# Attention in a fused decoder layer: where the value matmuls of a half are issued, and in which tile the last block's exponentials lie

## The chip, the core and the metric

The kernel runs on one core of one Trainium2 chip. The metric is the device time of one execution in microseconds, the median of several runs. Five engines work side by side, each in its own instruction order: TensorE (PE) for matmuls, VectorE (DVE), ScalarE (ACT) and GpSimd (POOL) for element-wise work, and SyncE (SP), which issues most DMAs. They wait for each other through semaphores.

## What is computed

One decoder layer on a sequence of 1024 tokens with 1024 channels: a state-space branch (SSD) and a latent-attention branch (MLA), merged by gates, then a gated feed-forward part. Everything is float32 in and out. The change touches the attention alone, which is, for 16 heads (64 value columns each, 96 query and key columns):

```python
def one_block(i):
    start = i * ATTN_Q_BLOCK
    qb = lax.dynamic_slice_in_dim(q, start, ATTN_Q_BLOCK, axis=1)
    s = jnp.einsum('bqhd,bkhd->bhqk', qb, k).astype(jnp.float32) * scale
    qpos = start + jnp.arange(ATTN_Q_BLOCK)
    s = jnp.where(qpos[:, None] >= key_pos[None, :], s, -jnp.inf)
    p = jax.nn.softmax(s, axis=-1).astype(v.dtype)
    return jnp.einsum('bhqk,bkhd->bqhd', p, v)
```

## The kernel before

The layer runs as stages one after the other: normalisation and small projections, the attention stage (about 105 to 697 us of the profiled execution), the SSD, the merge, the feed-forward part. In the attention stage PE's free places are filled with background work: the gate and z projections, whose matmuls write a PSUM tile `lin`. One background step is three lin matmuls of 512 columns (a product of two split numbers, high and low parts in fp32r). `advance(n)` issues n steps; `fill()` issues as many as the next digit of the table `PACE` says, so each call of `fill` uses up one place of the table. What is left of the background after the attention is issued by `flush()`.

Heads are worked in 8 pairs, and the 1024 queries in two halves of 512. A first half (half 0) has 4 key blocks of 128 keys, a second half 8. For each key block and head, `key_block` makes scores transposed (keys on the partitions, queries in the columns) with three matmuls into an `s` bank, adds the causal mask on DVE where the block is on the diagonal (L657), takes the exponential on ACT into a tile `e` (L659) and adds e to a running sum `acc`, head 0 on POOL, head 1 on DVE (L664). Of the last four blocks of a half, block number d (0 to 3) has only 512 - 128 d columns that count, so e is 512, 384, 256 and 128 columns wide. `values` then multiplies e with the values, one matmul for each head, both into one `pv` tile, head 0 in its upper 64 rows and head 1 in its lower ones (L670). These matmuls are plain float32 and 64 columns of the array wide. `output` adds acc over the partitions with a matmul against ones (L677), copies pv and the sums out on ACT and stores them by DMA from SP.

Ahead of the scores each pair needs its projections (`qkv_steps`, with a reciprocal square root in many small DVE instructions and the qk scalings L586 and L588), transposes to kh, kl, qh, ql (`qk_transposed`, L610 on PE, L613 on ACT, L614 on DVE) and the negative maxima of the scores (`maxima`: L627 matmuls, DVE reductions L629 and L632 into nm, mc at L637 or L639, and L643 matmuls). These are the side work: in a first half the second half's transposes and maxima, in a second half the next pair's projections, transposes and maxima. `aside` issues it by the counts of `SIDE`. All `s` tiles, those of the side work too, rotate through 4 PSUM banks; `e` tiles rotate through 6 buffers, of which the output's sums take one.

A finished key block goes on a queue. When the queue holds more than two blocks, `value_steps` takes the two oldest and issues their value matmuls; behind a half's last two it also issues the output. So the last two blocks of a half are multiplied after the first key block of the next half.

On PE the order of the program is the order of the code: a chain of order marks over all of PE's instructions fixes it. On the other engines a scheduler places instructions when the kernel is built, so that a changed PE order moves theirs too.

Of the kernel before, what the change touches and what calls it, by code (L numbers as in the profile page):

```python
# [9 lines left out]
F32 = mybir.dt.float32  # L10
F32R = mybir.dt.float32r
I32 = mybir.dt.int32
AF = mybir.ActivationFunctionType
ALU = mybir.AluOpType
# [3 lines left out]
P = 128  # L18
# [54 lines left out]
def tile_hybrid_layer(ctx: ExitStack, tc: tile.TileContext, x, cols, cons, w_main, w_small, w_uq, w_ukv,  # L73
                      w_ssd, w_mla, w_o, w_up, w_down, out, pace=PACE):
    nc = tc.nc
    V, S, G, PE = nc.vector, nc.scalar, nc.gpsimd, nc.tensor
# [130 lines left out]
    def advance(n):  # L207
        while n > 0 and background:
            r = next(background[0], None)
            if r is None:  # L210
                background.pop(0)
            elif not r:
                return
            else:
                n -= 1

    def fill():
        i = places[0]
        places[0] += 1
        advance(int(pace[i], 36) if i < len(pace) else 0)  # L220
# [216 lines left out]
    for half in range(2):  # L437
        for b in range(3):
            fill()
            ps = bps.tile([P, 512], F32, name="tps")  # L440
# [15 lines left out]
    for tab, c0 in ((rq, CG_QR), (rk, CG_KR)):  # L456
# [21 lines left out]
    e = bq.tile([P, NT, HEADS], F32, name="de")  # L478
    u = bq.tile([P, NT, HEADS], F32, name="du")
    V.tensor_tensor(v, sm[:, :, 0:32], cl[:, CG_DTB:CG_DTB + 32].unsqueeze(1).broadcast_to([P, NT, 32]),  # L480
                    op=ALU.add)
# [19 lines left out]
    ps = bps.tile([P, 512], F32, name="tps")  # L501
    PE.matmul(ps[:, 0:256], lhsT=tri, rhs=va, start=True, stop=True)
    S.copy(acum.rearrange("p t h -> p (t h)"), ps[:, 0:256])
    ps = bps.tile([P, 512], F32, name="tps")
# [11 lines left out]
    for half in range(2):  # L516
        fill()
        ps = bps.tile([P, 512], F32, name="tps")
# [7 lines left out]
    with tc.tile_pool(name="cp", bufs=2) as cp, tc.tile_pool(name="pss", bufs=4, space=PSUM) as pss, \  # L526
# [119 lines left out]

        def key_block(pr, half, j, hd, accs):

            c0 = max(0, j - 4 * half) * P
            w = 512 - c0  # L650
            qh, ql = qkvT[pr, half, hd, "q"]
            kh, kl = qkvT[pr, j // 4, hd, "k"]
            ks = slice((j % 4) * P, (j % 4 + 1) * P)
            ps = bank()
            mm3(ps[:, 0:w], (kh[:, ks], kl[:, ks]), (qh[:, c0:512], ql[:, c0:512]), True, True)
            if j >= 4 * half:
                V.tensor_tensor(ps[:, 0:P], ps[:, 0:P], negt, op=ALU.add)  # L657
            e = cp.tile([P, 512], F32, name="e", bufs=6)
            S.activation(e[:, c0:512], ps[:, 0:w], AF.Exp)  # L659
            if j == 0:  # L660
                accs.append(cp.tile([P, 512], F32, name="acc"))
                S.copy(accs[hd], e)
            else:
                (V if hd else G).tensor_tensor(accs[hd][:, c0:512], accs[hd][:, c0:512], e[:, c0:512], op=ALU.add)  # L664
            return e

        def values(pr, j, es, c0, pv, first, last):
            vt = qkv[pr][1]
            for hd in range(2):
                PE.matmul(pv[hd * 64:(hd + 1) * 64, c0:512], lhsT=vt[:, j, hd * 64:(hd + 1) * 64],  # L670
                          rhs=es[hd][:, c0:512], start=first, stop=last)

        def output(pr, half, accs, pv):

# [32 lines left out]
        def attention():  # L707


            for g, n in ((qkv_steps(0), 10), (transposes(0, 0), 4), (both(0, 0), 10)):  # L710
                for _ in range(n):
                    fill()
                    next(g, None)
            queue = []

            def value_steps():

                done = [queue.pop(0) for _ in range(2)]
                last = done[1][2] == 4 * done[1][1] + 3
                if last:  # L720
                    fill()
                for pr, half, j, es, pv, accs in done:
                    values(pr, j, es, max(0, j - 4 * half) * P, pv, j == 0, j == 4 * half + 3)
                if last:
                    output(pr, half, accs, pv)

            units = 0
            for pr in range(npair):
                for half in range(2):
                    if half == 0:  # L730
                        side = chain(transposes(pr, 1), both(pr, 1))
                    elif pr + 1 < npair:
                        side = chain(qkv_steps(pr + 1), transposes(pr + 1, 0), both(pr + 1, 0))
                    else:
                        side = iter(())
                    todo = iter(SIDE[half])

                    def aside():
                        for _ in range(next(todo)):
                            fill()  # L740
                            next(side, None)


                    pv = psv.tile([P, 512], F32, name="pv")
                    accs = []
                    for j in range(4 * half + 4):
                        es = []
                        for hd in range(2):
                            fill()
                            es.append(key_block(pr, half, j, hd, accs))  # L750
                            aside()
                        queue.append((pr, half, j, es, pv, accs))
                        units += 1
                        if units > 2:
                            fill()
                        if len(queue) > 2:
                            value_steps()
                        aside()
                    for _ in side:
                        fill()  # L760
            fill()
            fill()
            value_steps()

        attention()
        flush()
# [887 lines left out]
```

## Time and profile before

| | us |
|---|---|
| median of 3 timed runs | 2227.03 (2224.92 to 2229.38) |
| the profiled execution | 2224.44 |
| its span in the trace | 2222.6 |
| PE's granted clock in it | 0.996 |
| value matmuls (L670), busy | 72.9 in 384 records |
| scores in pieces of 512 columns, first matmul (L175), busy | 40.1 in 96 records |

In the timeline a row has the start in us, how long it lasted, engine, line, operation, output<-inputs, sizes, count, and in brackets how long the engine sat idle before it and for whom. Matmuls overlap in these records (the shown end of one lies behind the start of the next), so that the distance from start to start says what one costs. A plain float32 matmul appears as two records, so a group of four value matmuls has x8. A row of a wait table has the total in us, the times, and the longest.

### The profile page before, as it was taken

How to read it: one execution, taken by the hardware profiler on the slowest of the kernel's cores; microseconds unless marked ns; L12 is line 12 of the kernel's file. 1: busy time of each engine (PE TensorE's matmuls, PEld its weight loads, DVE VectorE, ACT ScalarE, POOL GpSimd, SP SyncE). 2: the span in 40 equal slices, each digit the busy share in tenths (PEclk: the TensorE clock that was granted, in tenths of full speed). 3: DMA queues.
4: the chain of work that ended last, by engine and by line, in shares of the span. 5: the costliest groups of instructions: out<-in, count | busy, mean ns of one | idle time of the engine just before them, and what ended most of it. 6: DMA issues, size and time to landing. Idle time of an engine off the chain costs nothing.

```text
span 2222.6 us, 31323 instructions
## 1 busy us (share of the span) xinstructions
PE 2173.7 (98%) x11488; PEld 1765.2 (79%) x11488; DVE 1430.4 (64%) x2496; ACT 1012.4 (46%) x1852; POOL 822.4 (37%) x911
## 2 busy tenths in 40 slices
PE   8999999999999999999999999999899999999999
PEld 6777777777777887878878889889688888888887
DVE  4466656666672469898876746546977777764432
ACT  5345454445444346666554424335544444443320
POOL 2244423443343237665455311012555555510000
PEclk9999999999999999999999999999999999999999
DMA  4121111111213224544276566543222222247531
GB/s 146 54 68 49 40 48 63 50 45 39 69 43 130 68 76 152 181 162 167 95 227 207 178 223 203 166 162 95 67 95 86 81 81 86 76 142 246 201 130 67
DMA packets 112714, 253.57 MB, mean 114 GB/s; under 512 B 13168, under 2 KB 19248, under 8 KB 112560
## 3 DMA queue, kind: packets, MB, share of 16 engines
q1 hardware_dynamic: 99008, 210.54, 28.6%
q0 software_dynamic: 11008, 37.76, 5.3%
q10 hardware_dynamic: 2544, 3.28, 0.4%
q8 instruction: 90, 1.47, 0.3%
q14 instruction: 64, 0.52, 0.1%
HBM read 194.63 MB, written 56.89 MB: 113 GB/s over the span
## 4 chain that ended last, share of the span: by engine, by line
PE 75%; DVE 13%; ACT 4%; DMA 3%; issue 2%; POOL 1%; SPq 0%; DVEq 0%; ACTq 0%; POOLq 0%
PE lin L175 12%; PE lin L177 12%; PE lin L176 12%; PE dps L177 8%; PE dps L175 8%; PE dps L176 8%; PE pv L670 2%; PE s L175 2%; PE s L176 1%; PE s L177 1%; PE s L627 1%; PE yp L891 1%; PE sn L874 1%; DMA wraw<-in_w_ssd 1%; DVE qk L588 1%
## 5 line engine op out<-in xcount | busy, mean ns | idle before, releaser
L175 PE MATMUL lin<-h,whi 128*128 128x512 f32 x1440 | 592.4, 411 | 0.0
L177 PE MATMUL lin<-h,wlo 128*128 128x512 f32 x1440 | 564.0, 392 | 0.0
L176 PE MATMUL lin<-h,whi 128*128 128x512 f32 x1440 | 563.0, 391 | 0.0
L175 PEld LDWEIGHTS lin<-h,whi 128*128 128x128 f32 x1440 | 271.4, 188 | 81.6 <-issue 33.4
L177 PEld LDWEIGHTS lin<-h,wlo 128*128 128x128 f32 x1440 | 270.7, 188 | 59.8 <-DVE wlo L154 0.2
L176 PEld LDWEIGHTS lin<-h,whi 128*128 128x128 f32 x1440 | 271.9, 189 | 53.2 <-issue 7.0
L153 ACT CAST whi<-wraw 128x512 fp32r<-128x512 f32 x276 | 166.6, 619 | 281.4 <-PE lin L176 131.6
L154 POOL TENSOR_TENSOR wlo<-wraw,whi 128x512 fp32r<-128x512 f32 x134 | 192.1, 1450 | 185.1 <-ACT whi L153 177.6
L659 ACT ACTIVATE e<-s 128x512 f32<-128x512 f32 (+1 forms) x192 | 93.7, 493 | 164.6 <-DVE s L657 137.7
L664 POOL TENSOR_TENSOR acc<-acc,e 128x512 f32<-128x512 f32 (+3 forms) x80 | 79.6, 995 | 230.8 <-ACT e L659 217.7
L154 DVE TENSOR_TENSOR wlo<-wraw,whi 128x512 fp32r<-128x512 f32 x142 | 99.2, 714 | 94.4 <-ACT whi L153 94.3
L154 DVE TENSOR_TENSOR h<-ar,h 128x1024 fp32r<-128x1024 f32 x40 | 48.7, 1225 | 108.8 <-ACT h L153 108.7
L850 ACT ACTIVATE seg<-abc,acum 128x128 f32<-128x128 f32 x256 | 80.6, 392 | 48.3 <-PE yp L891 42.3
L153 ACT CAST h<-ar 128x1024 fp32r<-128x1024 f32 x40 | 42.1, 1056 | 124.8 <-PE lin L176 115.7
L176 PE MATMUL dps<-wlo,h 128*128 128x512 f32 x240 | 93.4, 389 | 0.0
L175 PE MATMUL dps<-whi,h 128*128 128x512 f32 x240 | 93.4, 389 | 0.0
L177 PE MATMUL dps<-whi,h 128*128 128x512 f32 x240 | 93.4, 389 | 0.0
L812 DVE SCALAR_TENSOR_TENSOR xg<-craw,cl,xg 128x1024 f32<-128x1024 f32 x48 | 73.8, 1537 | 27.4 <-ACT xg L810 26.9
L664 DVE TENSOR_TENSOR acc<-acc,e 128x512 f32<-128x512 f32 (+3 forms) x80 | 53.5, 668 | 41.0 <-ACT e L659 40.4
L1140 ACT CAST xhi<-ur 128x512 fp32r<-128x512 f32 (+1 forms) x41 | 34.1, 832 | 89.5 <-PE dps L176 79.5
L670 PE MATMUL pv<-e,vt 128*64 128x512 f32 (+3 forms) x384 | 72.9, 499 | 0.0
L175 PE MATMUL s<-qh,kh 97*128 97x512 f32 (+1 forms) x192 | 68.5, 357 | 2.0 <-ACT qh L644 1.1
(587 smaller groups left out, 5189.5 us busy)
## 6 DMA issues: line engine op xcount, KB each, us to landing
wraw<-in_w_main SPq DMA_DIRECT2D x112, 256.0 KB, 3.1
ur<-in_w_up SPq DMA_DIRECT2D x44, 512.0 KB, 3.5
ar<-a_d SPq DMA_DIRECT2D x40, 512.0 KB, 5.1
abc<-ac_d POOLq DMA_DIRECT2D x32, 512.0 KB, 5.2
wraw<-in_w_ssd SPq DMA_DIRECT2D x64, 256.0 KB, 2.8
wraw<-in_w_down SPq DMA_DIRECT2D x44, 256.0 KB, 3.8
a_d<-uc SPq DMA_DIRECT2D x22, 512.0 KB, 2.6
g_d<-lt SPq DMA_DIRECT2D x32, 256.0 KB, 2.8
```

Source lines behind the costliest of these rows:

```text
L153: S.copy(hi, raw)
L154: (eng or V).tensor_sub(lo, raw, hi.bitcast(F32))
L175: PE.matmul(ps, lhsT=ah, rhs=bh, start=first, stop=False, **more)
L176: PE.matmul(ps, lhsT=ah, rhs=bl, start=False, stop=False, **more)
L177: PE.matmul(ps, lhsT=al, rhs=bh, start=False, stop=last, **more)
L588: V.tensor_tensor(qk[:, :, 2 + hd, 0:64], qk[:, :, 2 + hd, 0:64], rr[:, :, 2 + hd:3 + hd].broadcast_to([P, 4, 64]), op=ALU.mult)
L659: S.activation(e[:, c0:512], ps[:, 0:w], AF.Exp)
L664: (V if hd else G).tensor_tensor(accs[hd][:, c0:512], accs[hd][:, c0:512], e[:, c0:512], op=ALU.add)
L670: PE.matmul(pv[hd * 64:(hd + 1) * 64, c0:512], lhsT=vt[:, j, hd * 64:(hd + 1) * 64], rhs=es[hd][:, c0:512], start=first, stop=last)
L812: V.scalar_tensor_tensor(c, raw[:, k:k + T], col(cw + k), c, op0=ALU.mult, op1=ALU.add)
L850: S.activation(seg[:, hd, :], abc[:, hd, :], AF.Relu, bias=acum[:, c, 8 * g + hd:8 * g + hd + 1], scale=-1.0)
L1140: S.copy(hi, r)
```

## The change

The value matmuls are issued in other groups. A first half has one group with all four blocks at its end. A second half has groups after its third and fifth block (blocks 0 and 1, blocks 2 and 3) and one of its last four blocks at its end. The output follows the last group, so a half's output now stands ahead of the next half's first key block. In a second half `advance(1)` puts one more background step ahead of the last group, whatever the table says. The `fill` ahead of an output becomes a `fill` at a half's first block, so that the table's places meet the same points of the code as before; the two fills at the very end go.

The last block's e (128 columns) no longer takes a tile of its own. It goes into the first 128 columns of the second diagonal block's tile, of which that block uses only the other 384.

```diff
-            c0 = max(0, j - 4 * half) * P
+            d = max(0, j - 4 * half)
+            c0 = d * P
...
-            e = cp.tile([P, 512], F32, name="e", bufs=6)
-            S.activation(e[:, c0:512], ps[:, 0:w], AF.Exp)
+
+            if d < 3:
+                e = cp.tile([P, 512], F32, name="e", bufs=6)
+                if d == 1:
+                    shared.append(e)
+                e = e[:, c0:512]
+            else:
+                e = shared.pop(0)[:, 0:w]
+            S.activation(e, ps[:, 0:w], AF.Exp)
...
-            def value_steps():
-
-                done = [queue.pop(0) for _ in range(2)]
-                last = done[1][2] == 4 * done[1][1] + 3
-                if last:
-                    fill()
+            def value_steps(n):
+
+                done = [queue.pop(0) for _ in range(n)]
+                last = n == 4
...
-                        if len(queue) > 2:
-                            value_steps()
+                        if units > 4 and j == 0:
+                            fill()
+                        if half and j in (2, 4):
+                            value_steps(2)
                         aside()
                     for _ in side:
                         fill()
-            fill()
-            fill()
-            value_steps()
+                    advance(half)
+                    value_steps(4)
```

Lines behind the edit move: L657 is L658 in the changed kernel, L659 is L667, L664 is L672, L670 is L680 and L677 is L687.

First place: PE where pair 2's second half ends and pair 3's first half begins. Before, the last two blocks' values stand behind the next half's first key block and its transposes (L610):

```order
L610 MATMUL s<-cn,qk 97x128 x4
L175 MATMUL s<-qh_3604,kh_3563 128x512
L176 MATMUL s<-ql_3605,kh_3563 128x512
L177 MATMUL s<-qh_3604,kl_3564 128x512
L610 MATMUL s<-cn,qk 97x128 x4
L670 MATMUL pv<-e,vt 64x256 x2
L670 MATMUL pv<-e,vt 64x128 x2
L677 MATMUL s<-acc,cn 32x256 x4
L175 MATMUL lin<-h,whi 128x512
```

In the changed kernel the last key block (its s matmuls of 128 columns), one background step, and then all four blocks' values and the output's sums:

```order
L175 MATMUL s<-qh_3049,kh_3020 128x128
L176 MATMUL s<-ql_3050,kh_3020 128x128
L177 MATMUL s<-qh_3049,kl_3021 128x128
L175 MATMUL lin<-h,whi 128x512
L176 MATMUL lin<-h,whi 128x512
L177 MATMUL lin<-h,wlo 128x512
L680 MATMUL pv<-e,vt 64x512 x2
L680 MATMUL pv<-e,vt 64x384 x2
L680 MATMUL pv<-e,vt 64x256 x2
L680 MATMUL pv<-e,vt 64x128 x2
L687 MATMUL s<-acc,cn 32x256 x4
```

The values and the ones matmul have moved ahead of the next half, and the transposes there no longer have them as a neighbour.

Second place: DVE in pair 2's second half, where the next pair's ql (both heads, L614) and the qk scalings (L586, L588) meet. Before:

```order
L614 SCALAR_TENSOR_TENSOR ql_3587<-s,qg,qh_3586 97x512
L586 TENSOR_TENSOR qk<-qk,qrr 128x4x96
L588 TENSOR_TENSOR qk<-qk,qrr 128x4x64
L586 TENSOR_TENSOR qk<-qk,qrr 128x4x96
L588 TENSOR_TENSOR qk<-qk,qrr 128x4x64
L614 SCALAR_TENSOR_TENSOR ql_3605<-s,qg,qh_3604 97x512
L657 TENSOR_TENSOR s<-s,negt 128x128
```

In the changed kernel, at the same place:

```order
L586 TENSOR_TENSOR qk<-qk,qrr 128x4x96
L588 TENSOR_TENSOR qk<-qk,qrr 128x4x64
L586 TENSOR_TENSOR qk<-qk,qrr 128x4x96
L588 TENSOR_TENSOR qk<-qk,qrr 128x4x64
L614 SCALAR_TENSOR_TENSOR ql_3583<-s,qg,qh_3582 97x512
L658 TENSOR_TENSOR s<-s,negt 128x128
L614 SCALAR_TENSOR_TENSOR ql_3601<-s,qg,qh_3600 97x512
```

The first ql has moved behind the four scalings, and the second behind a mask addition too. In pair 4's second half the second ql has moved behind the scalings in the same way, and in pair 5's a product of the background (L330) no longer stands ahead of them.

Third place: PE in pair 3's first half, behind the third key block, among the maxima of the second half (L627). Before:

```order
L627 MATMUL s<-kh_3563,qh_3858 128x512
L627 MATMUL s<-kh_3811,qh_3858 128x256
L670 MATMUL pv<-e,vt 64x512 x2
L670 MATMUL pv<-e,vt 64x384 x2
L175 MATMUL lin<-h,whi 128x512
L176 MATMUL lin<-h,whi 128x512
L177 MATMUL lin<-h,wlo 128x512
L627 MATMUL s<-kh_3537,qh_3838 128x512
```

In the changed kernel:

```order
L627 MATMUL s<-kh_3559,qh_3859 128x512
L627 MATMUL s<-kh_3827,qh_3859 128x256
L175 MATMUL lin<-h,whi 128x512
L176 MATMUL lin<-h,whi 128x512
L177 MATMUL lin<-h,wlo 128x512
L627 MATMUL s<-kh_3547,qh_3839 128x512
```

The value group between the maxima is gone; only the background step is left between them.

More of the change, by code (lines that the diff above doesn't have):

```diff
@@ L663, in key_block @@
             else:
-                (V if hd else G).tensor_tensor(accs[hd][:, c0:512], accs[hd][:, c0:512], e[:, c0:512], op=ALU.add)
+                (V if hd else G).tensor_tensor(accs[hd][:, c0:512], accs[hd][:, c0:512], e, op=ALU.add)
             return e
+        shared = []
         def values(pr, j, es, c0, pv, first, last):
@@ L670, in values @@
                 PE.matmul(pv[hd * 64:(hd + 1) * 64, c0:512], lhsT=vt[:, j, hd * 64:(hd + 1) * 64],
-                          rhs=es[hd][:, c0:512], start=first, stop=last)
+                          rhs=es[hd], start=first, stop=last)
         def output(pr, half, accs, pv):
```

## The prediction, made before the changed kernel ran

> **What bounds the kernel now.** I read the page first (span, busy time, the chain that ended last), then the waits of TensorE (PE) inside the attention stage, then the timeline of PE around the value matmuls, and last the other engines' timelines there.
>
> ```profile
> span 2222.6 us, 31323 instructions
> PE 2173.7 (98%) x11488; PEld 1765.2 (79%) x11488; DVE 1430.4 (64%) x2496; ACT 1012.4 (46%) x1852; POOL 822.4 (37%) x911
> PE 75%; DVE 13%; ACT 4%; DMA 3%; issue 2%; POOL 1%; SPq 0%; DVEq 0%; ACTq 0%; POOLq 0%
> L175 PE MATMUL lin<-h,whi 128*128 128x512 f32 x1440 | 592.4, 411 | 0.0
> ```
>
> PE is busy for 98% of the span and is three quarters of the chain. The background matmuls (lin) never waited (0.0 in the last column), so a background step costs its PE time wherever it stands. What PE waits for in the attention stage (the window 150 to 730 us) is nearly all VectorE (DVE):
>
> ```profile
> PE s L627 <- DVE ql L614: 4.8, 4, 1.8
> PE s L643 <- DVE mc L639: 1.8, 4, 0.7
> PE s L643 <- DVE mc L637: 0.6, 1, 0.6
> PE s L175 <- DVE nm L632: 0.2, 1, 0.2
> ```
>
> The columns are total us, times, longest. So in this stage the time is the sum of PE's issue intervals, plus the places where DVE comes late. Both are touched by the change. I make the sum against the profiled execution (2224.44 us with a span of 2222.6) as a difference, and put it on the median of the three timed runs, 2227.03, which is 2.6 above that execution.
>
> **Term 1: fewer groups of value matmuls.** Before, a first half has two groups (blocks of 512 and 384 columns, then 256 and 128), a second half four (512 and 512 twice, 512 and 384, 256 and 128): 6 a pair, 48 in all. Now it is 1 and 3, 32 in all. No matmul is added or taken away, so what can go is what a group costs beside its columns.
>
> ```profile
> 352.62 0.28 PE L176 MATMUL s<-ql,kh 97*128 97x256 f32 x1
> 352.74 0.28 PE L177 MATMUL s<-qh,kl 97*128 97x256 f32 x1
> 352.95 1.73 PE L670 MATMUL pv<-e,vt 128*64 128x512 f32 x8
> 354.60 0.50 PE L175 MATMUL lin<-h,whi 128*128 128x512 f32 x1
> 354.94 0.39 PE L176 MATMUL lin<-h,whi 128*128 128x512 f32 x1
> 355.17 0.39 PE L177 MATMUL lin<-h,wlo 128*128 128x512 f32 x1
> ...
> 359.30 0.60 PE L610 MATMUL s<-cn,qk 128*97 128x128 f32 x4
> 359.83 0.87 PE L670 MATMUL pv<-e,vt 128*64 128x256 f32 x8
> 360.63 0.64 PE L677 MATMUL s<-acc,cn 128*32 128x256 f32 x8
> ...
> 340.12 1.94 PE L670 MATMUL pv<-e,vt 128*64 128x512 f32 x8
> 341.99 0.50 PE L175 MATMUL lin<-h,whi 128*128 128x512 f32 x1
> ```
>
> The starts (first column) are what counts, since the shown ends overlap. A 256-column s matmul normally starts 0.12 us after the one before it (352.62 to 352.74); the value group starts 0.21 after it: **0.09 to enter**. The first lin matmul behind the group lasts 0.34 until the next starts (354.60 to 354.94), the second 0.23: **0.11 after leaving**. Inside: 512+512 columns take 1.87 (340.12 to 341.99), 512+384 take 1.65, so 128 columns of both heads are 0.22, or 0.00172 us a column. 512+384 leaves 1.65 - 1.54 = 0.11 over, and 256+128 (359.83 to 360.63) 0.80 - 0.66 = 0.14. One group of 1280 columns should take 2.20 + 0.11 = 2.31 against 1.65 + 0.80 = 2.45: **0.14 inside**. Each of the 16 groups dropped thus saves 0.34: **-5.4 us**. Bounds: -2.2 if only the 0.14 goes, -5.8 if the last group's 0.14 goes in full.
>
> **Term 2: transposes lose a neighbour.** In PE's order of before, six of the 256+128 groups follow directly on transposes of the same plain float32 (359.30 above), which then leave to s or lin matmuls only once, together with the group. Now these transposes leave by themselves:
>
> ```profile
> 358.51 0.48 PE L175 MATMUL s<-qh,kh 97*128 97x512 f32 x1
> 358.83 0.40 PE L176 MATMUL s<-ql,kh 97*128 97x512 f32 x1
> 359.06 0.40 PE L177 MATMUL s<-qh,kl 97*128 97x512 f32 x1
> ```
>
> The s matmul behind four transposes lasts 0.32 until the next, the second 0.23, so 0.09 each, six times: **+0.6**, between 0 and 0.6.
>
> **Term 3: the last block's exponentials, and the sums.** The merged group now stands one background step behind the last s matmul of a second half, and the ones matmul (the sums) right behind the group. How late are e and acc today?
>
> ```profile
> 501.42 0.28 PE L177 MATMUL s<-qh,kl 97*128 97x128 f32 x1
> 503.07 0.28 ACT L659 ACTIVATE e<-s 128x128 f32<-128x128 f32 x1 [1.02 <-DVE s L657]
> 503.38 0.29 DVE L664 TENSOR_TENSOR acc<-acc,e 128x128 f32<-128x128 f32 x1 [0.21 <-ACT e L659]
> 211.83 1.28 POOL L154 TENSOR_TENSOR wlo<-wraw,whi 128x512 fp32r<-128x512 f32 x1
> 213.07 0.51 POOL L664 TENSOR_TENSOR acc<-acc,e 128x128 f32<-128x128 f32 x1
> ```
>
> This is the latest exponential of a second half: e is done 1.93 us and acc 2.25 us after that s matmul starts. The cover is 0.11 (the s matmul itself) + 0.69 (three lin matmuls of 0.23) + 0.09, then 1152 of the 1280 columns, 1.98: 2.87 us until the last block is wanted, 3.2 until the sums are. POOL's latest acc stood behind a weight split and ended at 213.58, 2.5 us after that half's last s matmul started (at 211.11 in PE's timeline). In a first half two minus-maximum groups (L643) and a step more lie between. So **0**; if that cover were gone, a second half would pay at most the 2.25 us, 8 times. The last block's exponentials in the second block's tile add no wait: that tile's free 128 columns were released with the tile. The output's copy and DMA now come before the next half's work in the queues of ScalarE and SyncE, and wait there for the group, with weight casts and loads behind them; the lin row's 0.0 says that such loads have room. The eight background steps done earlier (one a second half) only shorten the run of lin matmuls after the attention: 0, at most 8 x 0.69 = 5.5 if the next stage started late, of which I see no sign.
>
> **Term 4: where DVE now puts ql.** The second order fence of the change shows DVE at pair 2's second half. What this costs:
>
> ```profile
> 338.92 0.74 DVE L614 SCALAR_TENSOR_TENSOR ql<-s,qg,qh 97x512 fp32r<-97x512 f32 x1
> 340.85 0.42 DVE L588 TENSOR_TENSOR qk<-qk,qrr 128x256 f32<-128x256 f32 x1
> 339.97 0.22 PE L627 MATMUL s<-kh,qh 96*128 96x128 f32 x1
> ...
> 412.75 0.30 PE L627 MATMUL s<-kh,qh 96*128 96x128 f32 x1 [1.39 <-DVE ql L614]
> 559.67 0.39 PE L627 MATMUL s<-kh,qh 96*128 96x256 f32 x1 [1.78 <-DVE ql L614]
> 555.13 0.68 DVE L330 SCALAR_TENSOR_TENSOR lt<-lt,lin 128x512 f32<-128x512 f32 x1
> 633.50 0.39 PE L627 MATMUL s<-kh,qh 96*128 96x256 f32 x1 [0.34 <-DVE ql L614]
> ```
>
> In pair 2, ql ran at 338.92, ahead of the four qk scalings, and the maximum matmul at 339.97 did not wait. In pair 3 both ql stood behind the scalings, and PE waited 1.39. Pair 2 now has pair 3's order: +1.3. Pair 4 gets pair 6's order (one ql behind the scalings): +0.3. In pair 5 a background product (L330, 0.68) leaves the place ahead of the scalings: -0.6. Sum **+1.0**; bounds -1.8 (pair 5's wait gone, none new) and +3.6 (two as long as 1.78).
>
> The length of such a scaling is not fixed:
>
> ```profile
> 485.36 0.42 DVE L588 TENSOR_TENSOR qk<-qk,qrr 128x256 f32<-128x256 f32 x1
> 556.40 1.50 DVE L588 TENSOR_TENSOR qk<-qk,qrr 128x256 f32<-128x256 f32 x1
> ```
>
> The Trainium skill (GPSIMD Engine Reference, Specifications) says that GpSimd shares its memory interfaces with VectorE and that the two contend when a VectorE instruction has two inputs in SBUF. That would explain 1.50 against 0.42, and by it term 4 would be about +2 if the moved scalings met a weight split; the trace agrees as far as the two rows go.
>
> **Term 5: first halves lose cover.** The value group after a first half's third block stood in the middle of the maxima, which DVE reads out of PSUM; it is gone there (third order fence).
>
> ```profile
> 373.81 0.69 DVE L632 TENSOR_REDUCE nm<-s 128x1 f32<-128x512 f32 x1 [1.47 <-PE s L627]
> 379.10 0.46 DVE L637 TENSOR_TENSOR mc<-nm 128x4 fp32r<-128x4 f32 x1
> 379.31 0.31 PE L643 MATMUL s<-nid,mc 128*97 128x128 f32 x2
> ```
>
> PE reaches the end of the maxima 1.65 + 0.20 = 1.85 us sooner. DVE sat idle for 1.47 behind that group, waiting for PE, so it follows by 1.47. The rest, 0.4, is paid where the last maximum (mc, 379.10 + 0.46) is only just ready for L643; most other first halves have a lin step between. I take **+0.5** in all; bounds 0 and 8 x 1.85 = 14.8.
>
> **Sum.** -5.4 + 0.6 + 0 + 1.0 + 0.5 = -3.3 us: 2227.03 - 3.3 = **2223.7 us**.
>
> **The rivals.**
>
> *The cover holds* (no new wait; terms 4 and 5 at 0): -4.8, so 2222.2, and down to 2219 if pair 5's wait goes too and the waits on L643 shrink. For it: DVE is only 64% busy and the maxima's order on DVE is unchanged in the first halves. Against: DVE's own order of ql did change.
>
> *The group's price stays.* If the 0.09 and 0.11 belong to neighbours and come back at other seams, only 16 x 0.14 = 2.2 goes; with terms 4 and 5, 2227.03 - 2.2 + 1.5 = 2226.3. Against it: the 0.11 appears behind every kind of group shown above.
>
> *PSUM is read too slowly: slower than before.* Four s banks pass between PE, DVE and ScalarE; without the value group between them, PE in a first half waits for DVE to free a bank. If DVE does not follow at all, a first half pays 1.85 at its third block, less some 0.4 of room; 8 x 1.45 = 11.6, with terms 1, 2 and 4 together 2227.03 - 3.8 + 11.6 = 2234.8. It decides from 0.5 us a first half on. Against it is the idle 1.47. The Trainium skill (TensorEngine Tiling, PSUM Bottleneck) states that after a speedup of TensorE the copies out of PSUM may become the bottleneck; the row at 373.81, DVE waiting for PE, does not agree at that place.
>
> **How the numbers follow.** Chances: forecast 0.50 (its own range 2221.7 to 2226), cover holds 0.30, price stays 0.13, slower 0.07. A difference of 0.2% (4.45 us) is about what a measurement of this kernel can tell from no change, so faster means below 2222.6: most of the second case and a tenth from the forecast's lower end, 0.36; slower (over 2231.5) 0.06; within 0.58. The range 2219 to 2228.5 takes in the first three cases and leaves out the last and the tails.
>
> **What would show it.** 32 value groups, the merged one taking about 2.31 us from its start to the ones matmul, with the first lin behind the ones at 0.34; no wait of PE on e or acc at a half's end; a wait on ql of over 1 us in pair 2's second half; waits on mc of at most 0.4 in first halves. I am wrong if the merged group waits for its last block, if waits on nm or mc grow in every first half, or if the stage after the attention starts with a gap.

## The result, and the profile after

| | before | after |
|---|---|---|
| median of the runs compared, us | 2226.64 (2224.14 to 2229.38, 6 runs) | 2234.34 (2232.93 to 2241.0, 6 runs) |
| the profiled execution, us | 2224.44 | 2234.22 |
| its span, us | 2222.6 | 2232.4 |

The ratio is 1.0043 (95% interval 1.0032 to 1.0054): the changed kernel is slower, by 7.7 us between the medians. The forecast was 3.3 us faster, and the range ended at 2228.5.

The page of the changed kernel, the same lines as before (span, busy times, the chain that ended last, the background's first matmul):

```profile
span 2232.4 us, 31279 instructions
PE 2174.9 (97%) x11488; PEld 1766.7 (79%) x11488; DVE 1431.3 (64%) x2496; ACT 1011.6 (45%) x1852; POOL 819.6 (37%) x911
PE 73%; DVE 13%; ACT 6%; DMA 4%; issue 2%; POOL 1%; SPq 0%; ACTq 0%; DVEq 0%; POOLq 0%
L175 PE MATMUL lin<-h,whi 128*128 128x512 f32 x1440 | 591.8, 411 | 0.0
```

No engine's busy time grew by more than 1.5 us, and the background matmuls still wait for nothing. The span grew through time in which PE stands. What PE waits for in the attention stage (150 to 735 us) in the changed kernel, in total us, times, longest:

```profile
PE s L627 <- DVE ql L614: 6.0, 5, 1.8
PE s L610 <- DVE rsa L123: 3.2, 3, 1.9
PE s L643 <- DVE mc L639: 3.0, 6, 0.9
PE s L175 <- DVE kl L614: 1.8, 3, 0.6
PE s L627 <- DVE nm L632: 1.6, 2, 1.3
PE s L627 <- DVE nm L629: 1.4, 2, 0.8
```

Two rows of the same view before, which the prediction did not show:

```profile
PE s L610 <- DVE rsa L123: 1.6, 1, 1.6
PE s L627 <- DVE nm L632: 0.3, 1, 0.3
```

All rows of the view together went from 9.9 to 18 us, most of it on products of VectorE. The merged group itself is as expected; PE's timeline of the changed kernel, at the end of pair 2's second half, and (below the dots) at four places where PE waits:

```profile
358.22 2.37 PE L680 MATMUL pv<-e,vt 128*64 128x512 f32 x16
360.52 0.64 PE L687 MATMUL s<-acc,cn 128*32 128x256 f32 x8
361.09 0.50 PE L175 MATMUL lin<-h,whi 128*128 128x512 f32 x1
361.42 0.40 PE L176 MATMUL lin<-h,whi 128*128 128x512 f32 x1
...
341.54 0.30 PE L627 MATMUL s<-kh,qh 96*128 96x128 f32 x1 [1.46 <-DVE ql L614]
353.16 0.90 PE L643 MATMUL s<-nid,mc 128*97 128x128 f32 x8 [0.91 <-DVE mc L639]
376.09 0.44 PE L627 MATMUL s<-kh,qh 96*128 96x384 f32 x1 [0.84 <-DVE nm L629]
522.25 0.39 PE L627 MATMUL s<-kh,qh 96*128 96x256 f32 x1 [1.28 <-DVE nm L632]
```

From the group's start to the ones matmul 2.30 us (2.31 was forecast), behind the ones 0.33 to the next lin matmul (0.34). There is no wait on e or acc at a half's end. But each of the four waits below is 0.8 to 1.5 us on VectorE. Between 700 and 760 us PE has no wait at all, so the stage after the attention does not start with a gap.

To compare the kernels I worked out three sums from each trace. **Stage**: from the first key block's first scores matmul of pair 0 to one and the same matmul shortly behind the attention. **Issue**: the sum over PE's matmuls in it of the usual distance from start to start for that matmul between its two neighbours (lower quartile over the kernels). **Lateness**: by how much the distances exceed that, where it is more than 0.06 us, in the first halves and in the second (the ones left out). Some 10 us of smaller excesses remain in each kernel. Where matmuls of one shape that follow each other are taken as one, the change moves issue by -4.9 and lateness by +12.8, in place of the -5.7 and +13.5 below, so that differences of 1 us in these columns say little. Each kernel has one trace, and by two traces of nearly equal code (before and e1: 571.6 and 571.5) these sums repeat well (e12's issue is lower because the twelve matmuls of four steps stand ahead of its stage); the stages after the attention vary by several us from run to run, so that medians decide on the total.

### The profile page after: what moved, and what is told of

Same layout as the page of the kernel before. It is cut to its first block, busy times and chain, and to the rows that moved or that the text cites. A ratio compares the mean times of both kernels' runs of the same rounds, so it can differ in the third digit from the quotient of the medians.

```text
span 2232.4 us, 31279 instructions
## 1 busy us (share of the span) xinstructions
PE 2174.9 (97%) x11488; PEld 1766.7 (79%) x11488; DVE 1431.3 (64%) x2496; ACT 1011.6 (45%) x1852; POOL 819.6 (37%) x911
## 3 DMA queue, kind: packets, MB, share of 16 engines
q8 instruction: 90, 1.47, 0.3%
## 4 chain that ended last, share of the span: by engine, by line
PE 73%; DVE 13%; ACT 6%; DMA 4%; issue 2%; POOL 1%; SPq 0%; ACTq 0%; DVEq 0%; POOLq 0%
PE lin L175 12%; PE lin L176 12%; PE lin L177 12%; PE dps L177 8%; PE dps L175 8%; PE dps L176 8%; PE pv L680 2%; ACT e L667 1%; DMA wraw<-in_w_ssd 1%; PE s L627 1%; PE yp L900 1%; DVE acc L672 1%; PE sn L883 1%; PE s L175 1%; PE s L177 1%
## 5 line engine op out<-in xcount | busy, mean ns | idle before, releaser
L667 ACT ACTIVATE e<-s 128x512 f32<-128x512 f32 (+1 forms) x192 | 93.5, 493 | 170.3 <-DVE s L658 140.6
L672 POOL TENSOR_TENSOR acc<-acc,e 128x512 f32<-128x512 f32 (+3 forms) x80 | 79.3, 991 | 244.6 <-ACT e L667 211.8
L672 DVE TENSOR_TENSOR acc<-acc,e 128x512 f32<-128x512 f32 (+3 forms) x80 | 57.1, 714 | 39.3 <-ACT e L667 38.4
L658 DVE TENSOR_TENSOR s<-s,negt 128x128 f32<-128x128 f32 x128 | 38.3, 301 | 53.5 <-PE s L177 52.2
```

The lines of the kernel that those rows point to most:

```text
L667: S.activation(e, ps[:, 0:w], AF.Exp)
```

## The experiments

| run | median us (n) | ratio [95%] | stage | issue | late, first + second |
|---|---|---|---|---|---|
| before | | | 571.6 | 546.8 | 2.8 + 12.2 |
| after | 2234.34 (6) | 1.0043 [1.0032, 1.0054] | 579.9 | 541.1 | 8.5 + 20.0 |
| e1 | 2227.59 (10) | 0.9999 [0.9988, 1.0010] | 571.5 | 546.8 | 2.6 + 12.1 |
| e2 | 2234.16 (6) | 1.0037 [1.0021, 1.0052] | 581.0 | 543.8 | 6.5 + 20.4 |
| e3 | 2233.43 (10) | 1.0031 [1.0019, 1.0043] | 579.4 | 544.2 | 5.2 + 19.9 |
| e4 | 2236.59 (7) | 1.0042 [1.0030, 1.0055] | 581.2 | 541.5 | 8.6 + 21.0 |
| e5 | 2228.41 (10) | 1.0004 [0.9994, 1.0014] | 575.1 | 540.7 | 6.0 + 17.8 |
| e6 | 2234.00 (10) | 1.0029 [1.0019, 1.0038] | 578.2 | 546.9 | 4.0 + 17.6 |
| e7 | 2227.60 (10) | 1.0006 [0.9996, 1.0017] | 573.5 | 543.4 | 4.2 + 15.6 |
| e8 | 2226.73 (10) | 1.0000 [0.9986, 1.0013] | 572.5 | 540.7 | 5.9 + 15.5 |
| e9 | 2234.37 (10) | 1.0030 [1.0020, 1.0041] | 581.2 | 541.1 | 8.4 + 21.3 |
| e10 | 2226.62 (11) | 0.9998 [0.9989, 1.0007] | 573.9 | 541.0 | 7.8 + 14.8 |
| e11 | 2229.14 (11) | 1.0005 [0.9995, 1.0015] | 574.0 | 543.8 | 5.8 + 14.1 |
| e12 | 2235.14 (9) | 1.0032 [1.0021, 1.0043] | 581.6 | 544.1 | 2.9 + 24.5 |
| e13 | 2215.18 (5) | 0.9943 [0.9931, 0.9955] | 564.8 | 546.8 | 1.9 + 6.5 |
| e14 | 2217.45 (5) | 0.9949 [0.9937, 0.9961] | 569.0 | 546.9 | 1.5 + 11.1 |
| e15 | 2226.04 (11) | 0.9990 [0.9982, 0.9999] | 570.5 | 541.0 | 4.3 + 15.0 |
| e16 | 2227.89 (12) | 1.0000 [0.9992, 1.0009] | 571.2 | 546.8 | 1.9 + 12.8 |
| e17 | 2224.23 (12) | 0.9993 [0.9981, 1.0005] | 570.6 | 546.8 | 3.4 + 10.7 |
| e18 | 2222.66 (12) | 0.9985 [0.9975, 0.9995] | 571.0 | 541.0 | 3.7 + 16.1 |

Ratios are to the kernel before, run beside each on the same chip (its medians: 2225.68 to 2227.50). The change lowers issue by 5.7 us (546.8 to 541.1) and raises lateness by 13.5 (15.0 to 28.5): the gain came, and more than twice of it was lost to lateness, by the wait tables VectorE's for the most part. The experiments look for where that lateness comes from.

### The tile, and the first halves' groups

**e1**: the kernel before with the last block's e in the second block's tile, nothing else.

```diff
+            if d < 3:
+                e = cp.tile([P, 512], F32, name="e", bufs=6)
+                if d == 1:
+                    shared.append(e)
+                e = e[:, c0:512]
+            else:
+                e = shared.pop(0)[:, 0:w]
```

> The kernel before, with the last block's exponentials in the second diagonal block's tile and nothing else. Theory (lost cover: the value groups stood between matmuls whose PSUM banks VectorE and ScalarE must empty, and with them gone PE meets the same late VectorE sooner): the tile plays no part, so the time of before within 3 us, and PE's waits in the attention stage as before (15 us of lateness in the two kinds of halves together, 2.7 in first and 12.2 in second halves). Rival (the shared tile or the shorter rotation of e makes exponentials late): 3 us or more of the 8 to 10 appear here.

Ratio 0.9999: the tile plays no part.

**e2**: the changed kernel, with the value group of blocks 0 and 1 back behind a first half's third block.

```diff
-                        if half and j in (2, 4):
+                        if j == 2 or half and j == 4:
                             value_steps(2)
...
-                    value_steps(4)
+                    value_steps(4 if half else 2, True)
```

> The changed kernel, with the value group of blocks 0 and 1 put back behind a first half's third block (a first half has two groups again, the second at its end with the output). Theory (lost cover): a first half gets 1.65 us of cover back among its maxima and pays 0.34 for the extra group; its lateness falls from 8.4 us towards 4, second halves stay near 20; total 5 to 8 us over before. Rival (only the move of the output and of the last group matters, by ScalarE's queue or VectorE's order): lateness in first halves stays at 8 and the total rises by 2.7 to 10 to 12 over before.

**e3**: first halves grouped as before, so that only second halves have the merged group.

```diff
+                        if half and j == 0:
+                            value_steps(2, True)
+                        if j == 2 or half and j == 4:
                             value_steps(2)
...
+                    if half:
+                        value_steps(4, True)
```

> The changed kernel, with a first half as before: blocks 0 and 1 behind its third block, blocks 2 and 3 and the output behind the second half's first block. Only second halves have the merged group at their end. Theory (lost cover): second halves get 1.4 us of cover back ahead of the projections, their lateness returns from 20 to 12 to 14 us, first halves to 3 to 5; 8 groups fewer than before are worth 2.7; total -2 to +2 against before. Rival (the order on VectorE, ql behind the scalings, is what costs): total stays at +4 or more unless that order changes back too.

**e4**: a first half's group of four and its output behind the second half's first block.

```diff
+                        if half and j == 0:
+                            value_steps(4, True)
...
+                    if half:
+                        value_steps(4, True)
```

> The changed kernel, with a first half's one group of four and its output moved behind the second half's first block (head 1's third diagonal block shares a tile with head 0's, so that the e tiles suffice). All 16 groups stay dropped (-5.4). Theory (lost cover): second halves have 2.3 + 0.6 us of cover at their start, more than before, so their lateness is 12 or less; first halves keep 8 to 9; total -5.4 + 5.5 - 0 to 3, so -3 to +1 against before. Rival (merged groups make PE run ahead wherever they stand): +5 to +8, as the changed kernel.

Lateness of the first halves falls from 8.5 to 6.5 (e2) and 5.2 (e3), and issue rises by about 3 for the eight groups that are back; the total hardly moves, 2233.4 to 2236.6. The second halves stay at 20 us whatever the first do. So my first theory, that most of the loss was cover that the value groups had given, fell.

### The background step at a half's end

**e5**: the changed kernel without the extra step. **e6**: the kernel before with that step, and nothing else of the change.

```diff
# e5, against the changed kernel
-                    advance(half)
# e6, against the kernel before
+                    advance(half)
```

> The changed kernel without its extra background step (advance) ahead of a second half's last group. In its order VectorE has ql and the scalings where before had them; the value groups stand as in the changed kernel. Theory (phase: the eight extra steps shift the background against the attention, the scheduler then puts ql behind the scalings and a background product elsewhere, and second halves wait): lateness in second halves falls from 20 back to 12 to 14 us, first halves stay at 8 to 9; total 0 to +2 against before. Rival (lost cover in second halves): 20 us stay, total +6 or more.

> The kernel before plus one background step at the end of every second half; its value groups, tiles and table stand as before. No work is added, only eight steps are done sooner. Theory (phase): second halves go from 12 to about 20 us of lateness, first halves stay near 3; total +6 to +9 against before. Rival (the value groups are what counts): no change, within 2 us of before.

e6 alone costs 6.9 us (2234.00 against 2227.13), with every value group where it was. Without the step the changed kernel is back at 2228.41. The waits of PE in the kernel before with the step (e6), the same view as above:

```profile
PE s L627 <- DVE ql L614: 5.5, 5, 1.6
PE s L643 <- DVE mc L639: 3.0, 6, 1.0
PE s L610 <- DVE rsa L123: 2.9, 3, 1.6
PE s L627 <- DVE nm L632: 1.3, 1, 1.3
```

These are nearly the rows of the changed kernel (6.0, 3.0, 3.2, 1.6). The step itself is three matmuls earlier; but all that the background does afterwards (load, cast on ScalarE, split on GpSimd, product on VectorE) then falls on another point of the attention, and the program's order on VectorE follows: e6 has the changed kernel's order of ql and the scalings in all pairs.

**e7**: the changed kernel without the step, and with e2's group back in the first halves. **e8** and **e9**: the second half's rsqrt, scalings and rotation written behind the maxima, ahead of the seventh block, without the step (e8) and with it (e9). The scheduler then puts most scalings between and behind the ql; in no pair's second half does the first ql stand behind all four of them any more.

```diff
# e8 and e9
+                if pr and half:
+                    tails.append(tail)
+                else:
+                    tail()
...
+                        if j == 6 and tails:
+                            tails.pop()()
```

> The changed kernel without the extra step and with the group of blocks 0 and 1 back behind a first half's third block. Theory (phase in second halves, lost cover in first halves): second halves 12 to 14, first halves 5 to 6.5, ideal matmul time 3 less than before; total -1 to +2 against before. If cover in first halves counts for nothing: first halves 8 and total +3.

> The changed kernel without the extra step, and with the last part of a pair's projections (reciprocal square root, scalings and rotation of its second half, on VectorE and GpSimd) written behind the transposes and maxima, at the sixth block's end, where VectorE has less to do; PE's order is that of the kernel without the step. Theory (second halves wait because VectorE does the scalings ahead of ql): waits on ql fall from about 5 us to under 2, and the total is 3 to 5 us under the kernel without the step, so -5 to 0 against before. Rival (the ql waits come from the length of the transposes' own chain): waits on ql stay, and the total equals that kernel.

> The changed kernel, extra step included, with the last part of the projections written behind the maxima as in e8. Theory (the phase costs through ql standing behind the scalings on VectorE): waits on ql under 1 us, total down by 4 or more, to +1 to +4 against before. Rival (the phase costs through the whole chain on VectorE, whichever of its instructions is last): the waits move to mc, nm or e, the total stays at +5 to +8.

e7 and e8 are level with the kernel before (2227.60 and 2226.73), no better than e5 within the intervals. e9 takes away the waits on ql, and stays at 2234.37, though it differs from e8 by the step alone. Its largest waits (from here on, lines behind the edits have numbers higher by 5 to 8):

```profile
PE s L650 <- DVE mc L646: 4.7, 6, 2.1
PE s L634 <- ACT e L674: 2.2, 1, 2.2
PE s L617 <- DVE rsa L123: 1.9, 1, 1.9
PE s L634 <- DVE nm L639: 1.6, 2, 1.3
```

The time came back on the last maximum (mc, 3.0 to 4.7) and on e. That ql stands behind the scalings is thus where the lateness shows, not what makes it.

**e10**: the changed kernel, the extra step taken back at the next place of the table that has one, so that the background stands as before from there on. **e11**: the same with e2's group and e9's order. **e12**: the kernel before with the background moved by four steps once, ahead of the first pair.

```diff
# e10 and e11
+        n = int(pace[i], 36) if i < len(pace) else 0
+        if n and owed[0]:
+            n -= 1
+            owed[0] = 0
+        advance(n)
...
+                    owed[0] = half
# e12, against the kernel before
+            advance(4)
```

> The changed kernel, with the extra step ahead of a second half's last group taken back at the next place of the table that has a step, so that the background is in before's phase for the rest of each pair. Theory (phase): second halves 12 to 15 us of lateness with no wait on e at their end, first halves 6 to 8.5; ideal matmul time 5.7 less than before; total -2 to +2 against before. Rival (eight steps sooner cost by themselves, not by the phase): +5 or more.

> As e10, with the group of blocks 0 and 1 back in a first half's middle (8 groups dropped, not 16) and the last part of the projections written late. By the theory first halves 4 us, second halves 10 to 13, ideal matmul time 3 less than before: total -4 to 0 against before. If lateness only moves between waits: 0 to +2.

> The kernel before with four background steps done once, ahead of the first pair, and everything else as it was: the whole attention runs in another phase of the background. No work is added. Theory (phase): VectorE's order has ql behind the scalings in pairs 2 and 4, as in the changed kernel; second halves 15 to 20 us of lateness, total +3 to +7 against before. Rival (only steps done at a second half's end cost, as they delay the last value group): within 2 us of before.

e10 keeps the step as cover of the last block and is 7.7 us below the changed kernel: 2226.62, not to be told from the kernel before. e11 gains nothing more (2229.14). e12 moves no value group and costs 7.6 us. What is dear is where the background stands against the attention, not what was merged. (Only shifts to earlier steps were tried; whether one the other way costs as much is not shown.)

### Through what the shift costs

**e13** and **e14**: the kernel before, and e6, with the low part of the background's weights left out (the high part is used twice), so that GpSimd has no split of them.

```diff
# both; e14 has e6's step as well
-    def load_w(src, shape):
+    def load_w(src, shape, whole=True):
...
+        if not whole:
...
+                S.copy(hi[:, s, :].rearrange("p a b -> p (a b)"), raw)
+            return hi, hi
...
-        w = gate0[0] if ct == 0 else load_w(w_main[40 + ct], [P, KD, P])
+        w = gate0[0] if ct == 0 else load_w(w_main[40 + ct], [P, KD, P], False)
...
-        ws = [load_w(w_main[ct], [P, KD, P]) for ct in cts]
+        ws = [load_w(w_main[ct], [P, KD, P], cts[0] > 10) for ct in cts]
```

> The kernel before, with the background's low weight part left out (its gate and z tiles use the high part twice): GpSimd has no split of a background weight any more, the matmuls and ScalarE's casts stay. Theory 1 (the extra step costs time because the splits on GpSimd then fall beside the attention's small VectorE operations): with e14 beside it, e14 is at most 2 us above this run. Rival (the cost comes through VectorE's own order and the background's products, with no part of GpSimd): e14 stays 5 to 8 us above this run. Both: this run itself is 0 to 8 us below the kernel before, since some waits of the attention go.

> The same kernel as e13 with one more background step at the end of each second half, as in e6. Theory 1 (GpSimd's splits are the way): 0 to 2 us above e13. Rival (VectorE's order and the background's products): 5 to 8 us above e13, as e6 stands 6.9 us above the kernel before.

Without the splits the kernel is 11.9 us faster than before (e13; part of that lies ahead of the attention), and the step costs 2.3 us between medians (2215.18 to 2217.45) in place of 6.9. With five runs of each that 2.3 is uncertain by about 2 us, which still lies below 6.9. PE's waits in e13, then in e14:

```profile
PE s L635 <- DVE ql L622: 3.0, 3, 1.4
PE s L651 <- DVE mc L647: 0.6, 2, 0.3
```

```profile
PE s L635 <- DVE ql L622: 4.6, 4, 1.6
PE s L651 <- DVE mc L647: 0.6, 2, 0.3
PE s L618 <- DVE rsa L123: 0.5, 2, 0.3
```

e14 has the same order of ql on VectorE as e6, and waits 1.6 us more on ql than e13. But mc stays at 0.6 (1.8 to 3.0 from before to e6), and rsa rises to 0.5 only (1.6 to 2.9). By the medians the larger part of the shift's price goes with the splits; by the stage only a third of it does, which grows by 4.2 from e13 to e14 and by 6.6 from before to e6. And without the splits there is less lateness even where nothing is shifted (8.4 in e13, 15.0 before), so the shift may only meet more room there. How much of the price the splits make stays open. How a split can hold VectorE shows in the timeline of the kernel before, VectorE and GpSimd in pair 2:

```profile
333.04 0.17 DVE L119 TENSOR_SCALAR rsv<-qss 128x16 f32<-128x16 f32 x1
333.77 1.06 DVE L120 TENSOR_SCALAR qrr<-rsv 128x16 int32<-128x16 int32 x1
334.95 1.14 DVE L121 TENSOR_SCALAR qrr<-qrr 128x16 int32<-128x16 int32 x1
336.66 0.66 DVE L123 SCALAR_TENSOR_TENSOR rsa<-qrr,rsv 128x16 f32<-128x16 f32 x1
337.36 0.17 DVE L124 TENSOR_TENSOR rsa<-rsa,qrr 128x16 f32<-128x16 f32 x1
...
333.51 2.54 POOL L154 TENSOR_TENSOR wlo<-wraw,whi 128x512 fp32r<-128x512 f32 x2 [1.17 <-ACT whi L153]
336.01 1.29 POOL L664 TENSOR_TENSOR acc<-acc,e 128x512 f32<-128x512 f32 x1
```

An operation on 16 columns lasts 0.17 us with GpSimd idle (333.04). Beside the two splits and the acc it lasts 1.06, 1.14 and 0.66, and each ends as GpSimd's instruction does: at 334.83, 336.09 and 337.32, against 334.80, 336.06 and 337.29. In the stage 11 of 168 such operations (L119 to L125) last over 0.3 us, and all 11 end within 0.11 us of one of GpSimd's, 5 beside a split and 6 beside a sum (acc); 12 after the change, 6 in e13. The Trainium skill (SBUF — State Buffer, "SBUF: two separate sides") says that GpSimd's instructions and those of VectorE that have two inputs in SBUF, or run in a mode with two ports, take a shared pair of ports under an exclusive lock for the whole instruction, and that the other one blocks. The ends in these rows agree; L120 and L121 have one input each, and in which mode they ran no row shows.

But this stall does not make the shift dear. e6 has one such stall more than the kernel before (1.4 us in all), and e12, which pays 7.6 us, has three fewer. VectorE is busy for 358.3 us of the stage before, 363.0 in e6 and 358.6 in e12. What e12 has in common with e6 and the changed kernel is VectorE's order of ql and the scalings, and longer waits than before on ql (4.8) and mc (1.8):

```profile
PE s L627 <- DVE ql L614: 6.4, 5, 2.1
PE s L643 <- DVE mc L639: 3.7, 7, 1.0
```

That order is not the whole of it either: e9 pays without it, and e14 has it at a lower price. A split also delays what is queued behind it on GpSimd, acc and the rotations. By which way the shift costs time thus stays open.

**e17** (below as well) makes the same splits shorter, four pieces of 128 columns:

```diff
+            for c in range(0, n, P):
+                G.tensor_sub(lo[:, c:c + P], raw[:, c:c + P], hi[:, c:c + P].bitcast(F32))
```

> The kernel before, with each split of a weight on GpSimd written as four pieces of 128 columns in place of one of 512; nothing is left out. Theory 1 (a small VectorE operation that meets a split stands until GpSimd's instruction ends, so a shorter instruction gives it way sooner): lateness of the attention falls by 2 to 5 us, total 1 to 6 us below the kernel before. Rival (a waiting VectorE operation gets no turn between GpSimd's pieces, or the four pieces' longer total costs as much): within 1 us, or up to 5 us above.

1.5 us below the kernel before, with an interval that includes no change. The long operations became 18 of 168, shorter ones, 9.1 us over 0.17 in place of 11.1. Shorter instructions bring little.

### What the first halves pay

e10 still has 7.8 us of lateness in the first halves, against 2.8. VectorE's own waits (the view of VectorE's idle time, 150 to 735 us) show what was used up, before and after:

```profile
DVE nm L632 <- PE s L627: 15.4, 17, 1.6
DVE qk L566 <- ACT qk L565: 42.9, 27, 4.4
```

```profile
DVE nm L632 <- PE s L627: 5.1, 11, 0.9
DVE qk L566 <- ACT qk L565: 69.5, 29, 7.2
```

With the value group among the maxima VectorE waited 15.4 us for PE at the first row (L632 runs in first halves only), and now 5.1: the room at this place is gone. It is 14.3 in e6 and 3.7 in e5, so the groups took it and not the step. VectorE as a whole is not short of time: by the second row it now waits longer elsewhere. What the middle group alone is worth is shown by putting it back: lateness of the first halves falls by 2.0 (e2, from the changed kernel) and by 1.8 (e7, from e5), issue rises by 2.7 both times, and the medians move by less than 1 us. **e15** takes the second head's sums of the first halves off VectorE, in e10; **e16** does that in the kernel before.

```diff
-                (V if hd else G).tensor_tensor(...)
+                (V if hd and half else G).tensor_tensor(...)
```

> e10 (the changed kernel with the extra step taken back at the next place of the table) with the first halves' sums of the second head on GpSimd in place of VectorE. Theory (what e10 still loses in first halves is VectorE, which has no room once the value group in the middle is gone): lateness of first halves falls from 7.8 us to 4 to 6, total 2 to 4 us below the kernel before. Rival (GpSimd's extra work lengthens VectorE's operations, or the loss is TensorE's own order): within 1 us of e10, -2 to +1 against the kernel before.

> The kernel before with the same move of the first halves' sums to GpSimd and nothing else, to read e15 by. Theory (VectorE has room in first halves as long as the value group stands in the middle): within 1 us of the kernel before. Rival (VectorE is short of room there in any case): 2 to 4 us below it.

Lateness of e15's first halves falls to 4.3, and most of the waits on nm go with it. In e10:

```profile
PE s L632 <- DVE nm L634: 0.6, 1, 0.6
PE s L175 <- DVE nm L637: 0.6, 1, 0.6
PE s L632 <- DVE nm L637: 0.5, 2, 0.3
```

In e15 only this one is left:

```profile
PE s L175 <- DVE nm L637: 0.2, 1, 0.2
```

The total is 1.1 us below the kernel before, less than the 2 to 4 expected, and 1.9 below e16, which gains nothing; the two intervals overlap. In the first halves' lateness the move is worth 3.5 us behind the change (7.8 to 4.3) and 0.9 ahead of it (2.8 to 1.9): at the maxima VectorE had room before the change and lacks it after.

**e18** is e15 with e17's pieces.

> e15 (the changed kernel, its extra step taken back, the first halves' sums of the second head on GpSimd) with the splits in four pieces as in e17. Theory 1: 2 to 6 us below e15, so 3 to 7 us below the kernel before, a version ahead of both. Rival as in e17: within 1 us of e15, or above it.

2222.66, ratio 0.9985 [0.9975, 0.9995], 3.0 us below the kernel before, where the changed one stands 7.7 above it (each in its own comparison): a version ahead of both, by little.

## Why the prediction was wrong

| step | forecast us | measured us |
|---|---|---|
| terms 1 and 2, groups and transposes | -4.8 | -5.7 (issue; -4.9 with equal neighbours taken as one) |
| term 3, tile and last block | 0 | 0 (e1; no wait on e) |
| **term 3, eight background steps earlier** | **0** | **+6.9 (e6)** |
| term 4, ql behind the scalings | +1.0 | ql waits +1.2, within the 6.9 |
| term 5, cover of first halves | +0.5 | about +2 for the middle group (e2, e7); first halves in all +3.2 (e5) to +5.0 (e10) |
| sum | -3.3 | +4.4 to +6.2; the medians say +7.7 |

The measured rows come from different kernels, so their sum is rough, and it leaves out what second halves lose where the step is taken back (12.2 to 14.8 in e10), for which the forecast had term 4 alone.

**Terms 1 and 2** held: merged group and exit to 0.01 us, issue at most 0.9 lower than forecast. (The bound of -5.8 in term 1 does not come out of its rows; they give -5.4.) Eight groups give about half (e2 and e3, -3.0 and -2.6).

**Term 3** was right on the tile and on the last block's cover: without the step PE waits for e, but only a little, as e5 shows:

```profile
PE pv L680 <- ACT e L667: 0.6, 2, 0.4
```

The step that failed is the last one of term 3: "The eight background steps done earlier (one a second half) only shorten the run of lin matmuls after the attention: 0". I priced the step by its own matmuls and its end. But the step is also a shift: everything that comes due in the background by count of steps (casts, splits, products) moves against the attention's chain, and one shift by four steps ahead of the first pair is as dear as eight single ones (e12). With e6's 6.9 in its place the forecast would have been 3.6 us slower (2.6 without term 4, which the 6.9 contains). The bound of 5.5 there was for a late next stage, which did not happen.

**Term 4** was right in row and size: 1.46 in pair 2 (1.3 forecast), 4.8 to 6.0 in total. It did not say which part of the edit moves ql: the step does (e6 has the order), and not the merged groups (e5 does not). Taking the waits on ql out cures nothing (e9).

**Term 5** had the right mechanism and a size four to ten times too small. I took one half's 1.47 us of idle VectorE as cover in every half and priced the rest. That idle time was the slack of all eight: it fell from 15.4 to 5.1 us, and more of VectorE's delays then reach PE. The rival "PSUM is read too slowly" named this place, and its point of decision, 0.5 us a first half, was reached by the highest figure alone (5.0 us in 8 halves is 0.6, 3.2 is 0.4); but waits on nm grew at a few places only (0.3 to 3.0 us, of which e6 has 1.3), and it would not have made the kernel slower alone: e10 has it, and is level with the kernel before.

## What to carry to other kernels

When an edit moves even one step of interleaved background work, price it as a shift of all that comes after, not as the step: find which engine each background tile uses and where that lands on the waiting chain, or compensate the step at the next place. When a group of matmuls is taken out from between products that a second engine reads, compare what is saved with that engine's idle time summed over all such places. Test the edit's parts alone, each in the kernel before: one line of bookkeeping cost more here (6.9 us) than the merged groups saved (5.7).

## What was not expected of the hardware

VectorE operations on 16 columns last 0.17 us, and up to 1.31 us where GpSimd runs a split or a sum: they end when GpSimd's instruction ends. Cutting GpSimd's instructions in four makes such stalls more frequent and shorter (11 to 18, 11.1 to 9.1 us), with little effect on the time.
